# Six of eight experts with 64 slots and whole fp32 weights instead of four, expert 0 among them

## The chip, the core and the metric

The kernel runs on one core of a Trainium2 chip. The metric is the device time of one execution in microseconds (us), the median of several runs. Matrix products run on PE (TensorE), elementwise work on DVE (VectorE) and ACT (ScalarE); SP (SyncE) issues nearly all DMA transfers.

## What is computed

Two layers act on 256 context tokens and 256 image tokens, 1024 features wide. Each layer has a mixer and a feed-forward part; in the second layer only the image tokens go on, and their feed-forward part is a mixture of 8 experts of which each token uses two. The change touches this last part alone:

```python
def moe_swiglu(h, router, w1, w3, w2):
    t = h.reshape(-1, d)                                  # 256 tokens x 1024
    logits = t.astype(F32) @ router.astype(F32)
    top_logit, top_e = lax.top_k(logits, TOP_K)           # 2 of 8 experts
    gates = jax.nn.softmax(top_logit, axis=-1)
    ...
    # each expert, on the tokens that chose it: (silu(x @ w1) * (x @ w3)) @ w2
    out = jnp.zeros_like(t).at[slot_tok].add(ys * slot_gate[:, None].astype(t.dtype))
```

Per expert `w1` and `w3` are 1024 x 3584 and `w2` is 3584 x 1024, all fp32. On the given inputs the reference sends 53, 52, 64, 37, 43, 109, 114 and 40 tokens to experts 0 to 7.

## The kernel before

**Weights as a stream.** All weights come through a `Stream`: a list `todo` of blocks of 128 x 2048 fp32 (1 MB) in the order of use. `load` (L190) issues the DMA of the next block from SP's queue into a buffer; `fill` (L208) does so as long as the buffer at the head of a ring, `slots`, is free. In the expert part the ring has twelve buffers of 1 MB, and three more for a while: half of `xT` until block `n0 + LA_`, the tile `y` until block `n0 + LY`, and one that serves an earlier step. An expert has 42 blocks: 14 for each of `w1`, `w3` and `w2`, taken in units of `f` (512 of the 3584 columns), so eight experts have 336. SP has one queue: what stands behind a waiting instruction there waits too.

**Two kinds of expert.** A *big* expert has 128 slots for tokens. Its blocks are split: ACT copies a block to fp32r (`whi`, L246, two halves), DVE subtracts (`wlo`, L259, two halves), and PE multiplies in three passes with tokens on 128 columns: 12 matmuls of 512 columns a block (`up`, L1728 to L1731; `down`, L559 to L561). The raw buffer is free when both have read it. A *small* expert has 64 slots. Its blocks are not split: PE reads the raw block as fp32, two `f` or two halves of the output at once, one on the upper and one on the lower 64 columns of the array (L1719, L1753). Its raw buffer is free when PE has read it (`used`, L1706). In the profile one such fp32 matmul leaves two records.

**Who is what.** `CAP = (128, 64)` and `BIG = 4`: expert 0 always comes first, and its weights are addressed when the program is built, so they are loaded ahead; the other seven are sorted by token count on the chip, the three fullest are big, the rest small. The order is 0 (big), 4 (small), 1 (big), 5 (small), 2 (big), 6 (small), 3 (big), 7 (small), where from 1 on the number is the rank, not the expert. `gates` (L1609) ranks them on DVE after the router; `which_experts` (L1605) reads the seven numbers into SP registers, since later loads need them as addresses. If more tokens chose an expert than it has slots, `tc.If(most > 0)` (L1855) runs all experts once more as big ones, on the tokens that are left.

**The loop** (`moe`, L1661): in step n, `up` of unit n (`w1`, then `w3`), and `down` of unit n-1 (`w2`); in the last unit of an expert the tokens of the next are gathered with a 0/1 matrix (`gather`, L1677), and the result goes back through its transpose (`scatter`, L1764). A scheduler orders the instructions of each engine when the program is built.

Of the kernel before, what the change touches and what calls it, by code (L numbers as in the profile page):

```python
# [10 lines left out]
F32 = mybir.dt.float32  # L11
# [127 lines left out]
def program(tc, a, out):  # L139
# [14 lines left out]
    TAIL = (2, {1: 2, 2: 2}, {(1, 1), (2, 1), (3, 1), (4, 1)})  # L154
    NR, NH, LA = 2, 2, 1
    B4, B5 = 7, 3
    LY, LA_, NE_ = 37, 40, 5

    def bank(tag="m"):
        return ps.tile([128, 512], F32, name=nm("pm"), tag=tag, bufs=3 if tag == "m" else 1)  # L160
# [5 lines left out]
    class Halves:  # L166
# [5 lines left out]

        def __getitem__(self, i):
            return self.tiles[i[1] // self.rows][i[0], i[1] % self.rows, i[2]]

    class Stream:

# [86 lines left out]
        def take(self, la=None):  # L264
            la = LA if la is None else la
            i = self.pos[2]
            self.pos[2] += 1
            self.split_to(i + la)
            self.load_to(i + la + NR)
            self.fill()  # L270
            src, n, split, shape = self.todo[i]
            p = self.parts.pop(i)
            if not split:
                return p[:, :n].rearrange("p (j c) -> p j c", j=shape[0]) if shape else p[:, :n]
            return tuple(Halves(t, *shape) for t in p)
# [46 lines left out]
        want(*colblk('cd_w_out', c0, 256))  # L322


    CAP = (128, 64)
    BIG = 4
    SEQ = [(0, False), (4, True), (1, False), (5, True), (2, False), (6, True), (3, False), (7, True)]
    which = {}

    def units_of(seq):  # L330
# [1179 lines left out]
        V.tensor_scalar(dg, ident, rs[:, t:t + 1], None, op0=OP.mult)  # L1510
        TE.matmul(pb[:, t * 128:(t + 1) * 128], ones, dg, start=True, stop=True)
    tick(T2, False)
    pw, ww = bank(), ws.parts[n0][0][0]
    rt = ep.tile([128, 8, 8], F32, name="rt")
    nc.gpsimd.dma_start(rt, a['router'].rearrange("p (k e) -> p k e", k=8))
    cst = nw.tile([128, NROW], F32, name="cst", tag="row", bufs=1)
# [81 lines left out]
    slots, gts = [small_tile(2, 8) for i in range(2)]  # L1598
    P.iota(io64, pattern=[[0, 2], [1, 64]], base=0, channel_multiplier=0, allow_small_or_imprecise_dtypes=True)

    P.memset(lim, 8.0 * CAP[1] + 7)
    P.memset(lim[:, :BIG], 8.0 * CAP[0] + 7)
    P.memset(lim[:, 0:1], 8.0 * CAP[0] + 1e6)

    def which_experts(columns):  # L1605
        for x in columns:
# [54 lines left out]
    def moe(st, units, slots, main):  # L1661
# [15 lines left out]
        def gather(x, small):  # L1677
            sel, selr = st_q[x]
            if small:
                xe = ep.tile([128, KD, 64], F32, name=nm("xs"), tag="xe")  # L1680
                p = bank()
                for k in range(KD):
                    for i in range(2):
                        for t in range(2):
                            TE.matmul(p[:, k * 64:k * 64 + 64], h2[i][:, t, k * 128:(k + 1) * 128], selr[:, t, :64],  # L1685
                                      start=i == 0 and t == 0, stop=i == 1 and t == 1)
                A.activation(xe, p.rearrange("p (k s) -> p k s", k=KD), AF.Copy)
            else:
                xe = ep.tile([128, 2, KD, 128], F32R, name=nm("xe"), tag="xe")
                xe = [xe[:, 0], xe[:, 1]]  # L1690
                for i in range(2):
                    p = bank2()
                    for k in range(KD):
                        for t in range(2):
                            TE.matmul(p[:, k // 4, (k % 4) * 128:(k % 4) * 128 + 128], h2[i][:, t, k * 128:(k + 1) * 128],  # L1695
                                      selr[:, t, :], start=t == 0, stop=t == 1)
                    src = p.rearrange("p b (k s) -> p (b k) s", k=4)
                    (V.tensor_copy(xe[i], src) if x == 0 and i else A.activation(xe[i], src, AF.Copy))
            sT = nw.tile([128, 2, 128], F32 if small else F32R, name=nm("sT"), tag="stg" if small else "sc", bufs=1)
            p = bank()  # L1700
            for t in range(2):
                TE.transpose(p[:, t * 128:(t + 1) * 128], sel[:, t, :], ident)
            A.activation(sT, p[:, :256].rearrange("p (t s) -> p t s", t=2), AF.Copy)
            xe_q[x], st_q[x] = xe, sT

        def used():  # L1706

            st.done = st.pos[2]
            st.fill()

        def up(x, small, fs):
            p = bank()
            if small:
                n = 256 * len(fs)
                for hf in range(2):
                    w = [st.take(0) for _ in fs]
                    for k in range(4):
                        for j in range(2):
                            TE.matmul(p[64 * j:64 * j + 64, :n], xe_q[x][:, 4 * hf + k, :],  # L1719
                                      w[j][:, k, :] if len(fs) > 1 else w[0][:, k, j * 256:j * 256 + 256],  # L1720
                                      start=hf == 0 and k == 0, stop=hf == 1 and k == 3)
                    used()
                return p
            for hf in range(2):
                bh, bl = st.take()
                xh, xl = [x[:, 4 * hf:4 * hf + 4, :] for x in xe_q[x]]
                for k in range(4):
                    TE.matmul(p, xh[:, k, :], bh[:, k, :], start=hf == 0 and k == 0, stop=False)  # L1728
                    TE.matmul(p, xh[:, k, :], bl[:, k, :], start=False, stop=False)  # L1729
                for k in range(4):  # L1730
                    TE.matmul(p, xl[:, k, :], bh[:, k, :], start=False, stop=hf == 1 and k == 3)  # L1731
            return p
# [13 lines left out]
        def down(x, small, fs, at, first, last):  # L1746
            for hf in range(2 * len(fs)):
                if small:
                    w = st.take(0)
                    for i in range(2):  # L1750
                        half, c = (hf // 2, 2 * (hf % 2) + i) if len(fs) > 1 else (hf, i)
                        for j in range(2):
                            TE.matmul(ys[x][64 * j:64 * j + 64], at[:, c, 64 * half:64 * half + 64], w[:, i, j * 512:(j + 1) * 512],  # L1753
                                      start=first and hf == 0 and i == 0, stop=last and hf == 2 * len(fs) - 1 and i == 1)
                    used()
                    continue
                bh, bl = st.take()
                for i in range(2):
                    for j in range(2):
                        c = slice(j * 512, (j + 1) * 512)  # L1760
                        mm3(ys[x][j], at[0][:, 2 * hf + i, :], at[1][:, 2 * hf + i, :], bh[:, i, c], bl[:, i, c],
                            first and hf == 0 and i == 0, last and hf == 1 and i == 1)
# [52 lines left out]
        for n in range(len(units) + 1):  # L1815
            if n < len(units):
                x, small, fs, first, last = units[n]
                w = 256 * len(fs) if small else 512
                p1 = up(x, small, fs)
                s = nw.tile([128, 512], F32, name=nm("es"), tag="sq", bufs=3)  # L1820
                A.activation(s[:, :w], p1[:, :w], AF.Silu)
            if n:
                at = tr(prev, units[n - 1][1], 2 * len(units[n - 1][2]) if units[n - 1][1] else 4)
            for _ in range(min(2 if n and units[n - 1][1] else 1, len(due))):
                scatter(*due.pop(0))
            if n < len(units):
                p3 = up(x, small, fs)
                V.tensor_tensor(s[:, :w], s[:, :w], p3[:, :w], op=OP.mult)  # L1828
                if last and x in after:
                    gather(*after[x][:2])  # L1830
            if n:
                px, psmall, pfs, pfirst, plast = units[n - 1]
                if pfirst:
                    p = bank2()
                    ys[px] = p[:, 0, :] if psmall else [p[:, 0, :], p[:, 1, :]]
                down(px, psmall, pfs, at, pfirst, plast)
                if plast:
                    evac(px, psmall)
                    due += [(px, psmall, t, j) for t in range(2) for j in range(2)]
                if main and px == 0:  # L1840
                    if pfs[0] == 1:
                        gate_cols()
                    if pfs[0] == 2:
                        which_experts(range(1, NE))
                    if pfs[0] == 5:
                        sums()
                if (2 if psmall else 4) in pfs and px in after:
                    pick(*after[px][:2], slots)
            prev = s if n < len(units) else None
# [4 lines left out]
    most = nc.values_load(cnti[0:1, 0:1], min_val=0, max_val=8 * S)  # L1854
    with tc.If(most > 0):  # L1855

        V.tensor_scalar(slots[:, :, :BIG], slots[:, :, :BIG], float(CAP[0]), None, op0=OP.subtract)
        V.tensor_scalar(slots[:, :, BIG:], slots[:, :, BIG:], float(CAP[1]), None, op0=OP.subtract)
        st = Stream()
        rest = units_of([(x, False) for x in range(NE)])  # L1860
        moe_entries(st, rest, {0: 0})
        st.slots = [[slot_wp, -1, None] for _ in range(NR)] + [[slot_ep, -1, None] for _ in range(NE_)]
        st.fill()
        moe(st, rest, slots, False)
    ctx.close()


# [14 lines left out]
```

## Time and profile before

| | |
|---|---|
| median of 3 runs | 1786.39 us (1781.04 to 1786.47) |
| profiled execution, its own time | 1785.85 us |
| span, first to last instruction | 1783.6 us |
| busy in the span | PE 95%, DVE 55%, ACT 43%, POOL 7% |
| read from HBM | 471.40 MB, 266 GB/s over the span |
| mean granted TensorE clock | 0.983 |

The span is smaller than the execution's time by 2.25 us, which lie around it. PE's busy share says little by itself, because matmuls overlap: the expert part begins at about 885 us and must be read from the transfers and the waits in it.

### The profile page before, as it was taken

Reading aid. Unit: us, or ns where it says so; the run is one execution under the profiler, and the core shown is the slowest. Engines: PE = TensorE matmul, PEld = TensorE weight load, DVE = VectorE, ACT = ScalarE, POOL = GpSimd, SP = SyncE. Lnnn points to the kernel's source line nnn. Section 1 sums busy time; section 2 is a strip of 40 time slices with the busy share of each in tenths; the row PEclk is TensorE's granted clock in tenths of the full one; section 3 lists DMA queues with packets and bytes.
Section 4 is the critical chain, followed back from the end, with each engine's and each line's share of the span. In section 5 each row is a group of like instructions: output and inputs, shape, how many; then the busy total and the mean of one; then the engine's idle time right before and its main releaser. Section 6 shows DMA issues by size and latency. Waiting matters only on the chain. (4 is left out here: it accounts for less than half of the span.)

```text
span 1783.6 us, 22575 instructions
## 1 busy us (share of the span) xinstructions
PE 1700.4 (95%) x8669; PEld 1165.6 (65%) x8669; DVE 975.3 (55%) x1401; ACT 759.8 (43%) x1061; POOL 122.5 (7%) x87
## 2 busy tenths in 40 slices
PE   6898899999999998899989999999999999999997
PEld 2685577887777776777768744676446764467633
DVE  6688856333333247677678712885217852188521
ACT  3465734222221234544567602665126751267510
POOL 1433300000000000520100000000000000000000
PEclk9998999999999999999999999999999999999999
DMA  9534325223234233552879699998999979999897
GB/s 355 191 129 144 130 86 200 96 92 118 106 106 147 96 115 137 212 191 100 348 283 356 244 422 424 425 423 314 425 425 423 396 296 424 425 423 412 303 424 311
DMA packets 78739, 476.09 MB, mean 267 GB/s; under 512 B 8400, under 2 KB 12880, under 8 KB 29408
## 3 DMA queue, kind: packets, MB, share of 16 engines
q1 hardware_dynamic: 76000, 468.25, 66.8%
q0 software_dynamic: 1536, 5.28, 0.8%
q8 instruction: 70, 1.15, 0.3%
q10 hardware_dynamic: 1088, 1.05, 0.2%
q14 instruction: 45, 0.37, 0.1%
HBM read 471.40 MB, written 3.15 MB: 266 GB/s over the span
## 5 line engine op out<-in xcount | busy, mean ns | idle before, releaser
L259 DVE TENSOR_TENSOR wlo<-raw,whi 128x1024 fp32r<-128x1024 f32 (+2 forms) x414 | 487.2, 1213 | 254.3 <-ACT whi L246 245.4
L246 ACT ACTIVATE whi<-raw 128x1024 fp32r<-128x1024 f32 (+2 forms) x447 | 453.5, 1048 | 342.5 <-PE pm L560 116.4
L1719 PE MATMUL pm<-raw,xs 128*64 128x512 f32 (+1 forms) x1024 | 209.5, 542 | 0.0
L1729 PE MATMUL pm<-wlo,xe 128*128 128x512 f32 x448 | 183.8, 410 | 6.0 <-DVE wlo L259 6.0
L1728 PE MATMUL pm<-whi,xe 128*128 128x512 f32 x448 | 176.1, 398 | 4.9 <-ACT whi L246 4.9
L1719 PEld LDWEIGHTS pm<-raw,xs 128*64 128x64 f32 x1024 | 73.3, 137 | 118.7 <-issue 108.8
L1731 PE MATMUL pm<-whi,xe 128*128 128x512 f32 x448 | 123.3, 397 | 0.0
L259 POOL TENSOR_TENSOR wlo<-raw,whi 128x1024 fp32r<-128x1024 f32 (+1 forms) x33 | 80.1, 2440 | 577.5 <-ACT k L1218 486.4
L1729 PEld LDWEIGHTS pm<-wlo,xe 128*128 128x128 f32 x448 | 84.3, 188 | 45.6 <-DVE wlo L259 17.9
L1828 DVE TENSOR_TENSOR es<-es,pm 128x512 f32<-128x512 f32 (+1 forms) x44 | 29.0, 660 | 153.9 <-PE pm L1719 135.6
L1753 PE MATMUL p<-raw,ats 128*64 128x512 f32 x448 | 105.7, 597 | 0.5 <-ACT ats L1740 0.5
L1728 PEld LDWEIGHTS pm<-whi,xe 128*128 128x128 f32 x448 | 84.5, 189 | 24.7 <-ACT whi L246 8.2
L559 PE MATMUL pm<-hhi,whi 128*128 128x512 f32 x240 | 96.1, 406 | 3.8 <-ACT hhi L547 3.8
L560 PE MATMUL pm<-hlo,whi 128*128 128x512 f32 x240 | 97.3, 405 | 1.5 <-DVE hlo L548 1.4
L1731 PEld LDWEIGHTS pm<-whi,xe 128*128 128x128 f32 x448 | 84.7, 189 | 20.7
L561 PE MATMUL pm<-hhi,wlo 128*128 128x512 f32 x240 | 96.4, 402 | 0.0
L560 PE MATMUL p<-wlo,ath 128*128 128x512 f32 x224 | 92.5, 413 | 0.2 <-DVE wlo L259 0.2
L559 PE MATMUL p<-whi,ath 128*128 128x512 f32 x224 | 90.0, 402 | 0.7 <-ACT ath L538 0.7
L559 PE MATMUL p<-hhi,whi 128*128 128x512 f32 x224 | 89.0, 398 | 1.3 <-ACT hhi L538 0.7
L561 PE MATMUL p<-whi,atl 128*128 128x512 f32 x224 | 89.3, 398 | 0.0
L560 PE MATMUL p<-hlo,whi 128*128 128x512 f32 x224 | 89.1, 398 | 0.0
L561 PE MATMUL p<-hhi,wlo 128*128 128x512 f32 x224 | 88.8, 396 | 0.0
(443 smaller groups left out, 2686.6 us busy)
## 6 DMA issues: line engine op xcount, KB each, us to landing
raw<-in_moe_w_dram SPq DMA_DIRECT2D x331, 1024.0 KB, 12.1
rm<-in_mod_w_dram SPq DMA_DIRECT2D x96, 512.0 KB, 4.8
raw<-in_ffn_w_dram SPq DMA_DIRECT2D x30, 1024.0 KB, 4.8
raw<-in_ab_w_in_dram SPq DMA_DIRECT2D x7, 1024.0 KB, 6.8
raw<-in_cd_w_in_dram SPq DMA_DIRECT2D x6, 1024.0 KB, 6.5
raw<-in_ab_w_out_dram SPq DMA_DIRECT2D x4, 1024.0 KB, 4.9
raw<-in_cd_w_out_dram SPq DMA_DIRECT2D x4, 1024.0 KB, 4.9
raw<-in_ffn_w_dram SPq DMA_DIRECT2D x4, 768.0 KB, 4.2
```

The source lines that it names most:

```text
L246: x = A.activation(h, c, AF.Copy)
L259: x = low.tensor_tensor(l, r, h.bitcast(F32), op=OP.subtract)
L559: TE.matmul(p, wh, xh, start=first, stop=False)
L560: TE.matmul(p, wh, xl, start=False, stop=False)
L561: TE.matmul(p, wl, xh, start=False, stop=last)
L1719: TE.matmul(p[64 * j:64 * j + 64, :n], xe_q[x][:, 4 * hf + k, :], w[j][:, k, :] if len(fs) > 1 else w[0][:, k, j * 256:j * 256 + 256], sta ...
L1728: TE.matmul(p, xh[:, k, :], bh[:, k, :], start=hf == 0 and k == 0, stop=False)
L1729: TE.matmul(p, xh[:, k, :], bl[:, k, :], start=False, stop=False)
L1731: TE.matmul(p, xl[:, k, :], bh[:, k, :], start=False, stop=hf == 1 and k == 3)
L1753: TE.matmul(ys[x][64 * j:64 * j + 64], at[:, c, 64 * half:64 * half + 64], w[:, i, j * 512:(j + 1) * 512], start=first and hf == 0 and i = ...
L1828: V.tensor_tensor(s[:, :w], s[:, :w], p3[:, :w], op=OP.mult)
```

## The change

Expert 0 becomes small, and of the other seven only the two fullest are big: `CAP = [64, 128, 128, 64, 64, 64, 64, 64]`, in the order 0 (small), 3 (small), 1 (big), 4 (small), 2 (big), 5, 6, 7 (small). The limits for the second pass follow, and the second pass itself gets two rounds, since expert 0 can now have up to 256 - 64 tokens left. `Strips` lets PE read an unsplit block that lies in `xT`, in strips of 256 columns. `LY` and `LA_` change the blocks up to which `y` and `xT` serve as buffers. `gate_cols` and `which_experts` come after expert 0's first unit instead of its second and third. The first block is no longer split ahead of the router.

```diff
-    LY, LA_, NE_ = 37, 40, 5
+    LY, LA_, NE_ = 83, 39, 5
...
+    class Strips:
+        def __init__(self, x, shape):
+            self.x, self.n = x, shape[1] // S
+
+        def __getitem__(self, i):
+            c0, c1, _ = i[2].indices(self.n * S)
+            return self.x[i[0], i[1] * self.n + c0 // S:i[1] * self.n + c1 // S, :]
...
+            if not split and len(p.shape) == 3:
+                return Strips(p, shape)
...
-    CAP = (128, 64)
-    BIG = 4
-    SEQ = [(0, False), (4, True), (1, False), (5, True), (2, False), (6, True), (3, False), (7, True)]
+    BIG = 2
+    CAP = [64] + [128] * BIG + [64] * (7 - BIG)
+    SEQ = [(x, CAP[x] == 64) for x in (0, 3, 1, 4, 2, 5, 6, 7)]
...
-    pw, ww = bank(), ws.parts[n0][0][0]
+    pw, ww = bank(), ws.parts[n0]
...
-    P.memset(lim, 8.0 * CAP[1] + 7)
-    P.memset(lim[:, :BIG], 8.0 * CAP[0] + 7)
-    P.memset(lim[:, 0:1], 8.0 * CAP[0] + 1e6)
+    P.memset(lim, 8.0 * 64 + 7)
+    P.memset(lim[:, 1:BIG + 1], 8.0 * 128 + 7)
+    P.memset(lim[:, 0:1], 8.0 * 64 + 1e6)
...
-            sT = nw.tile([128, 2, 128], F32 if small else F32R, name=nm("sT"), tag="stg" if small else "sc", bufs=1)
+            sT = nw.tile([128, 2, 128], F32 if small else F32R, name=nm("sT"), tag="stg" if small and x != x0 else "sc", bufs=1)
...
+        def mm64(o, x, w, start, stop):
+            TE.matmul(o if len(w.shape) == 2 else o.rearrange("p (a b) -> p a b", b=S), x, w, start=start, stop=stop)
...
                 if main and px == 0:
-                    if pfs[0] == 1:
+                    if pfs[0] == 0:
                         gate_cols()
-                    if pfs[0] == 2:
                         which_experts(range(1, NE))
-                    if pfs[0] == 5:
+                    if pfs[0] == 4:
                         sums()
...
-        V.tensor_scalar(slots[:, :, :BIG], slots[:, :, :BIG], float(CAP[0]), None, op0=OP.subtract)
-        V.tensor_scalar(slots[:, :, BIG:], slots[:, :, BIG:], float(CAP[1]), None, op0=OP.subtract)
...
+        for columns, gone in ((range(NE), CAP), ([0], [128])):
```

Three places in the instruction order are needed below. A tile's name carries a number that differs from build to build.

SP's queue where expert 0 begins, before: after the first blocks of the expert part, five more loads stand ahead of the register loads of `which_experts` (L1607).

```order
L200 DMA raw_6838<-in_moe_w_2048_dram 128x2048
L200 DMA raw_7091<-in_moe_w_2048_dram 128x2048
L200 DMA raw_7113<-in_moe_w_2048_dram 128x2048
L200 DMA raw_7138<-in_moe_w_2048_dram 128x2048
L200 DMA raw_7160<-in_moe_w_2048_dram 128x2048
L200 DMA raw_7184<-in_moe_w_2048_dram 128x2048
L1607 TENSOR_LOAD cst
L1607 ISA x2
```

The same place in the changed kernel (its L1619 is L1607 of before, L210 is L200). `raw_6828` is the last block that needs no buffer to come free, the 14th; before it was `raw_6838`, the 15th.

```order
L210 DMA raw_6828<-in_moe_w_2048_dram 128x2048
L1619 TENSOR_LOAD cst
L1619 ISA x2
...
L210 DMA raw_7079<-in_moe_w_2048_dram 128x2048
L210 DMA raw_7081<-in_moe_w_2048_dram 128x2048
L1619 TENSOR_LOAD cst
L1619 ISA x2
L1868 TENSOR_LOAD cnti
L1868 ISA x2
L210 DMA raw_7091<-in_moe_w_2048_dram 128x2048
```

Six of the seven register loads now stand ahead of the 15th block's load, the seventh and that of `cnti` ahead of the 17th's.

DVE at the same place, before: the ranking of the experts (L1612 to L1627) stands between the splits of expert 0's blocks.

```order
L1617 TENSOR_TENSOR oh<-oh,g_6968 128x32
L259 TENSOR_TENSOR wlo_7133<-raw_6539,whi_7131 128x1024
L1618 TENSOR_TENSOR gt<-oh 128x16
L1621 SCALAR_TENSOR_TENSOR cst<-pm_6981,cst 128x8
L259 TENSOR_TENSOR wlo_7154<-raw_6541,whi_7152 128x1024
L1622 TENSOR_SCALAR cst<-cst 128x1
L259 TENSOR_TENSOR wlo_7155<-raw_6541,whi_7153 128x1024
L1623 MAX cst<-cst 128x8
```

The same instructions in the changed kernel:

```order
L1629 TENSOR_TENSOR oh<-oh,g_6958 128x32
L1630 TENSOR_TENSOR gt<-oh 128x16
L1633 SCALAR_TENSOR_TENSOR cst<-pm_6971,cst 128x8
L1634 TENSOR_SCALAR cst<-cst 128x1
L1635 MAX cst<-cst 128x8
L1636 MAX_INDEX cst<-cst 128x8
L1637 CAST cst<-cst 128x8
L1638 CAST cst<-cst 128x8
```

The splits between them are gone; the second cast writes the numbers that SP reads.

PE at the change from expert rank 5 to rank 6 in the changed kernel, small to small, which the kernel before does not have (L1714 transposes the 0/1 matrix for the next scatter, L1783 is the scatter of a small expert, L1724 all its other matmuls):

```order
L1714 MATMUL pm_10813<-ident,sel_10720 128x128 x2
L1724 MATMUL p_1920_10603<-raw_10679,ats_10753 64x512 x4
L1752 MATMUL pm_10868<-ident,es_10746 128x128 x2
...
L1783 MATMUL pm_10948<-zt_10911,sT_10379 128x512
L1783 MATMUL pm_10951<-zt_10911,sT_10379 128x512
...
L1783 MATMUL pm_11039<-zt_10911,sT_10379 128x512
L1783 MATMUL pm_11042<-zt_10911,sT_10379 128x512
```

The scatter of rank 5 still reads `sT_10379` after the transposes of rank 6 are made, and both lie in the one buffer `stg`; so `pm_10813`, one of three PSUM banks, is held until the last of these scatters.

## Rows read from the trace of the kernel before

**Rows 1.** The page: DMA rate in 40 equal slices of the span.

```profile
GB/s 355 191 129 144 130 86 200 96 92 118 106 106 147 96 115 137 212 191 100 348 283 356 244 422 424 425 423 314 425 425 423 396 296 424 425 423 412 303 424 311
```

**Rows 2.** Windows: length; PE, PEld, DVE, ACT, POOL busy; clock; DMA share; GB/s.

```profile
890.00:1030.00 140.00, 134.09 (x613) 101.85 (x613) 107.50 (x131) 94.26 (x108) 0.00 (x0) 0.98 0.79 297
1030.00:1200.00 170.00, 165.94 (x766) 99.85 (x763) 85.69 (x87) 73.09 (x85) 2.55 (x2) 1.00 1.01 424
1200.00:1255.00 55.00, 53.90 (x251) 35.14 (x250) 30.67 (x31) 28.25 (x33) 0.00 (x0) 1.00 0.85 334
...
1395.00:1485.00 90.00, 90.00 (x404) 62.51 (x404) 59.24 (x58) 49.88 (x58) 0.00 (x0) 1.00 0.87 347
...
1635.00:1715.00 80.00, 80.00 (x360) 51.38 (x358) 45.59 (x44) 39.90 (x47) 2.56 (x2) 1.00 0.89 350
```

**Rows 3.** Timeline of PE: expert 0 begins, then first small expert.

```profile
881.16 3.79 PE L1695 MATMUL p<-selr,h 128*128 128x128 f32 x32
...
885.17 0.48 PE L1728 MATMUL pm<-whi,xe 128*128 128x512 f32 x1
...
1018.00 13.95 PE L1719 MATMUL pm<-raw,xs 128*64 128x512 f32 x64
1031.88 0.50 PE L559 MATMUL p<-whi,ath 128*128 128x512 f32 x1
...
1037.35 0.40 PE L561 MATMUL p<-whi,atl 128*128 128x512 f32 x1
...
1053.13 7.04 PE L1753 MATMUL p<-raw,ats 128*64 128x512 f32 x32
```

**Rows 4.** Timeline of PE: the third and the fourth small expert begin.

```profile
1459.20 1.07 PE L1719 MATMUL pm<-raw,xs 128*64 128x512 f32 x2
...
1681.26 1.07 PE L1719 MATMUL pm<-raw,xs 128*64 128x512 f32 x2
```

**Rows 5.** Loads of L200 in windows 880:960, 1085:1135, 1200:1240, one row each.

```profile
DMA to landing us min/median/max: 4.7/4.9/6.7
...
DMA to landing us min/median/max: 19.2/19.6/19.7
...
DMA to landing us min/median/max: 4.7/5.6/6.8
```

**Rows 6.** Groups by line from 885 us on: busy us, mean ns, idle before.

```profile
L259 DVE TENSOR_TENSOR wlo<-raw,whi 128x1024 fp32r<-128x1024 f32 x328 | 385.5, 1220 | 99.2 <-ACT whi L246 96.5 <-PE pm L1731 2.1
L246 ACT ACTIVATE whi<-raw 128x1024 fp32r<-128x1024 f32 x328 | 331.3, 1052 | 101.4 <-PE pm L1731 83.2 <-PE p L561 13.1 <-DMA raw<-in_moe_w_dram 3.1
...
L1687 ACT ACTIVATE xs<-pm 128x512 f32<-128x512 f32 x4 | 2.3, 578 | 0.0
```

**Rows 7.** Timelines of ACT, then DVE, at the routing.

```profile
885.23 0.39 ACT L1703 ACTIVATE sT<-pm 128x256 fp32r<-128x256 f32 x1 [0.95 <-PE pm L1702]
...
889.87 1.28 ACT L1613 ACT_TABLE_LOAD   x1
...
878.44 0.17 DVE L1572 CAST ixf<-ix 128x4 f32<-128x4 uint32 x1
878.64 0.19 DVE L1573 TENSOR_TENSOR oh<-cst,ixf 128x32 f32<-128x32 f32 x1
```

**Rows 8.** Line L1607: duration ns min/median/max, first and last start.

```profile
L1607 SPq TENSOR_LOAD <-cst x7: 262/271/489, 902.7 to 907.5; - x7
```

**Rows 9.** Line L198, the last two blocks' loads in halves.

```profile
L198 SPq DMA_DIRECT2D raw<-in_moe_w_dram x4: 333/333/333, 1748.8 to 1756.0; - x4
...
DMA to landing us min/median/max: 15.4/17.2/18.9
```

**Rows 10.** Windows, columns as in Rows 2: end of the second small expert.

```profile
1310.00:1325.00 15.00, 14.42 (x106) 7.92 (x104) 0.90 (x3) 3.56 (x6) 0.00 (x0) 1.00 1.01 421
1325.00:1330.00 5.00, 2.78 (x13) 0.72 (x9) 1.26 (x2) 2.62 (x4) 0.00 (x0) 1.00 1.02 429
1330.00:1335.00 5.00, 4.98 (x15) 3.78 (x16) 3.59 (x4) 2.85 (x4) 0.00 (x0) 0.66 1.02 429
```

More of the change, by code (lines that the diff above doesn't have):

```diff
@@ L1718, in up @@
                         for j in range(2):
-                            TE.matmul(p[64 * j:64 * j + 64, :n], xe_q[x][:, 4 * hf + k, :],
-                                      w[j][:, k, :] if len(fs) > 1 else w[0][:, k, j * 256:j * 256 + 256],
-                                      start=hf == 0 and k == 0, stop=hf == 1 and k == 3)
+                            mm64(p[64 * j:64 * j + 64, :n], xe_q[x][:, 4 * hf + k, :],
+                                 w[j][:, k, :] if len(fs) > 1 else w[0][:, k, j * 256:j * 256 + 256],
+                                 hf == 0 and k == 0, hf == 1 and k == 3)
                     used()
@@ L1752, in down @@
                         for j in range(2):
-                            TE.matmul(ys[x][64 * j:64 * j + 64], at[:, c, 64 * half:64 * half + 64], w[:, i, j * 512:(j + 1) * 512],
-                                      start=first and hf == 0 and i == 0, stop=last and hf == 2 * len(fs) - 1 and i == 1)
+                            mm64(ys[x][64 * j:64 * j + 64], at[:, c, 64 * half:64 * half + 64], w[:, i, j * 512:(j + 1) * 512],
+                                 first and hf == 0 and i == 0, last and hf == 2 * len(fs) - 1 and i == 1)
                     used()
@@ L1855, in program @@
     with tc.If(most > 0):
-        V.tensor_scalar(slots[:, :, :BIG], slots[:, :, :BIG], float(CAP[0]), None, op0=OP.subtract)
-        V.tensor_scalar(slots[:, :, BIG:], slots[:, :, BIG:], float(CAP[1]), None, op0=OP.subtract)
[L1859 to L1864, printed above, removed]
+        for columns, gone in ((range(NE), CAP), ([0], [128])):
+            for x in columns:
+                V.tensor_scalar(slots[:, :, x:x + 1], slots[:, :, x:x + 1], float(gone[x]), None, op0=OP.subtract)
+            st = Stream()
+            rest = units_of([(x, False) for x in columns])
+            moe_entries(st, rest, {0: 0})
+            st.slots = [[slot_wp, -1, None] for _ in range(NR)] + [[slot_ep, -1, None] for _ in range(NE_)]
+            st.fill()
+            moe(st, rest, slots, False)
     ctx.close()
```

## The prediction

> **What bounds the kernel now.** I read the page's slices first, then windows of the expert part, then what PE needs for one block, and last what keeps a transfer from being issued.
>
> The slices show three regimes [rows 1]. Up to slice 19 (some 850 us) the rate is mostly 90 to 210 GB/s: that part waits for arithmetic, and the change hardly touches it. From there on the rate sits at 422 to 425 GB/s in most slices, with dips to 244, 314, 296 and 303. The windows put numbers on them [rows 2]. From 1030 to 1200 the transfers run at 424 GB/s without a break while PE counts as busy for 165.94 of 170 us. So in the expert part the weights are the limit, and time is lost only where the rate dips. A stretch loses its length times (1 - rate/424): 41.9 us in 890 to 1030, 11.7 in 1200 to 1255, 16.3 in 1395 to 1485, 14.0 in 1635 to 1715, together 83.9 us.
>
> Why it dips is seen in PE's price of a block. At 424 GB/s one block (1024 KB, 1.049 MB) lands every 2.473 us, an expert (42 blocks) in 103.9 us. A big expert has 12 matmuls per block; 23 steps between 1031.88 and 1037.35 make 0.238 us each [rows 3], so 2.85 us a block and 120 us an expert. A small one takes 13.95 us for the 8 blocks of the two `up` of a unit and 7.04 for the 4 of `down` [rows 3], 1.75 us a block, 73.5 us an expert, and gathers, transposes and scatters on top. A big expert is slower than its weights, a small one faster. While a big one runs, loaded blocks pile up until no buffer is free. The landing time shows it: at the end of the first small expert a load waits 19.6 us in a deep queue; as the next big one ends, 4.7 to 6.8 us, so hardly a load is ahead of it [rows 5]. A small expert then works the pile off. From one small expert to the next it takes 222.06 us [rows 4] where the weights of two need 207.7: the dip of 14 us again. The first 41.9 us are the same thing from a worse start: expert 0 is big and begins with all buffers full.
>
> **The change, part by part.** The sum is made against the profiled execution: 1785.85 us, a span of 1783.6 and 2.25 around it; the median, 1786.39, is 0.03% above. I sum when the last block lands, and add what follows it.
>
> *Start.* In SP's order 14 blocks are loaded before anything must come free (15 before, since the first was split early). PE gathers expert 0's tokens from 881.16 for 3.79 us, to 884.95 [rows 3], with as many matmuls as before. Their evacuation takes 0.58 us [rows 6], so the first `up` begins near 885.9 instead of 885.17. After two blocks, 3.5 us, two buffers are free: 889.4. But on SP six register loads now stand ahead of the 15th load and wait for the ranking. That comes after the exponential of the gates, for which ACT does the evacuation, 0.39 us for `sT`, 1.28 us of table load [rows 7] and a short activation: 887.4. DVE's chain of some 12 small instructions steps by 0.20 us [rows 7], which gives 889.8; no split stands between them any more. The seven register loads begin between 902.7 and 907.5 [rows 8]: six steps in 4.8 us, with a transfer issued among them, so some 0.7 us each; six take 4.2 us: 894.2. The first load then lands after 4.7 us in an empty queue [rows 5], at 898.9. Behind the waiting SP stand only weight loads; PE, at 1.75 us a block, comes to the 15th at 885.9 + 24.5 = 910.4, so nobody waits. Bounds: without the wait the first load goes at 889.4, 4.8 us earlier; a start as bad as now is priced among the rivals.
>
> *The blocks left.* 336 - 14 = 322, so 321 follow the first at 2.473 us: 793.8 us. Without a dip the last lands at 1692.7.
>
> *The dips.* Two big experts are left, each after a small one that has drained the pile, as in the three dips of before. Each costs 11.7 to 16.3; I take the mean of the three, 14.0: 28.0 us. At the lower end nothing, if the buffers hold the surplus. The last landing is at 1720.7.
>
> *Small after small.* Here 30 us of slack per expert (103.9 against 73.5) cover PE's other work. The one new wait: `sT` of the next expert must wait for the last scatters of the one before, and one of three PSUM banks is held so long. It can cost PE a few waits for DVE, within the slack; so 0. Without the slack the nearest row is a gather, 3.79 us [rows 3], for each of two such changes, 8 us.
>
> *Splits.* An expert made small drops 84 copies on ACT (1.052 us) and 84 subtractions on DVE (1.220 us) [rows 6], 88 and 102 us. They ran beside PE and the transfers; taking them away is worth nothing by itself beyond the start above.
>
> *`LY`, `LA_`, order of the side work.* Buffers that serve longer or shorter ahead of the first big expert, where transfers are the limit anyway: 0. The wider second pass is code that does not run.
>
> *Tail.* Before, the last half block was issued at 1756.0 and took 15.4 us [rows 9]: it landed at 1771.4, 12.2 us before the end. The last expert is small in both, so 12.2 again: a span of 1732.9, and with 2.25 a time of **1735 us**, 2.8% less.
>
> *A rule against it.* The row has 424 GB/s for 170 us [rows 2]. "DMA: Bandwidth & Descriptors" of the Trainium skill gives in its section Specifications a limit of about 358 GB/s from HBM for one core. By that figure a block would take an estimated 2.93 us, 321 of them 940 us, and the sum would come to some 1881 us, slower than before. The trace contradicts it for this kernel with one core at work, so the row decides, and I give that outcome no chance.
>
> **The rivals.**
>
> *No dips.* The starved smalls leave all buffers empty when a big expert begins, and its surplus, 42 x (2.85 - 2.473) = 16 us or 6 to 7 blocks, fits in twelve buffers. Then 28 us are saved on top: **1707 us**. Against it: the queue was at its deepest, 19.2 to 19.7 us, before the dip at 1200 too [rows 5], and the dip came.
>
> *The start or the starved experts lose more.* In 890 to 1030 my start loses what passes before the first block's 2.473 us begin, 896.4 - 890 = 6.4 us. If expert 0 loses 41.9 again [rows 2], 35 us come back: **1770 us**, and anything from 1748 on if small experts keep the queue less full than one did in 1030 to 1100. For it: they hold each buffer from issue to use, and take two at a time. Against it: the queue grew deeper all through the small experts of before [rows 5].
>
> *PE's clock.* Five of six small experts now wait for nearly every pair of blocks. In the trace the granted clock was full, 1.00, in 1310 to 1325 with PE busy for 14.42 of 15 us; after 1325 to 1330, with PE busy for 2.78 of 5 us, it fell to half, for 0.66 over the next 5 us [rows 10]. At 1.2 GHz a small expert's 73.5 us become 147, some 43 above its weights. A lost stretch here and there gives **1750 to 1780**; the gain of 51 is gone when the clock stays down for about 1.2 whole experts, and more makes it slower. Against it: a PE at half rate no longer waits, and after the row at 0.66 the clock was back. "TensorE: Matmul & The Clock Gate" of the Trainium skill, section "HAM oscillation — how this bites in real kernels", says that waits for transfers between groups of matmuls can bring the clock down again and again; the trace shows this one fall [rows 10] and 1.00 in the windows of 1030 to 1255 [rows 2], so no oscillation yet.
>
> *The second pass runs.* Expert 2 gets 64 tokens by the reference, exactly its slots, and is third of the seven. One token chooses it third, 0.0018 in the logit behind its second choice, where logits spread by 4.7. If the chip's arithmetic turns that, 65 tokens overflow 64 slots, and nine big experts follow, at 120 us or more: about **2815 us**. Before, expert 2 was big. Nothing in the trace speaks for such an error, and little can exclude it.
>
> **How the numbers follow.** 0.69 for the forecast, by itself 1724 to 1746 (dips of 9 to 18 each, start 5 either way); 0.09 for no dips; 0.10 for more lost; 0.08 for the clock, of which 0.02 slower; 0.04 for the second pass. The range 1712 to 1757 leaves out about 0.08 below (no dips) and 0.12 above. A difference of 0.3%, 5.4 us, is about what a measurement of this kernel can tell: faster 0.93, same 0.01, slower 0.06.
>
> **What would show it.** Right: weights at 424 GB/s from about 900 to 1150; two dips of some 14 us, at the ends of the two big experts; the register loads at about 890; no split of a block (L246 and L259 of before) between 885 and 1050; the last block landing near 1721 and the end 12 us later; PE less busy, with idle time put down to loads. Wrong: a dip at the start or between small experts, a granted clock under 0.97 after 1000, matmuls of three passes at the end of the program (the second pass), or no dips at all.

## The result and the profile after

The changed kernel takes **1731.8 us** (1729.69 to 1735.54, 4 runs) against 1786.43 (1781.04 to 1786.77, 4 runs), a ratio of 0.9703 [0.9678, 0.9729]: 3.0% less, where 2.8% (1735 us) was forecast. The profiled execution has a span of 1728.9 us (before 1783.6) and a mean granted clock of 0.985.

The page's slices of the changed kernel, the answer to [rows 1], DMA rate in 40 slices of the span:

```profile
GB/s 352 200 122 171 122 98 196 85 98 122 110 110 113 117 94 143 199 199 97 304 287 419 424 424 423 425 424 334 424 424 425 399 299 425 423 425 424 425 423 287
```

The weak slice after the start of the expert part is shorter, and two dips are left, 334 and 399 with 299, where there were three. In windows, the columns as in [rows 2]:

```profile
900.00:1030.00 130.00, 121.10 (x600) 47.90 (x596) 9.52 (x19) 11.27 (x21) 0.00 (x0) 1.00 1.02 421
1030.00:1150.00 120.00, 114.12 (x515) 74.94 (x516) 72.86 (x71) 62.73 (x70) 0.00 (x0) 0.99 1.01 424
1150.00:1185.00 35.00, 35.00 (x167) 28.08 (x166) 29.20 (x28) 23.92 (x26) 0.00 (x0) 1.00 1.00 409
1185.00:1220.00 35.00, 33.90 (x148) 18.10 (x146) 11.76 (x13) 10.28 (x14) 0.00 (x0) 1.00 0.83 327
...
1340.00:1390.00 50.00, 50.00 (x214) 38.25 (x212) 42.25 (x41) 35.51 (x39) 0.00 (x0) 1.00 0.99 394
1390.00:1420.00 30.00, 30.00 (x147) 23.37 (x148) 20.99 (x22) 16.71 (x20) 0.00 (x0) 1.00 0.90 320
1420.00:1500.00 80.00, 78.90 (x388) 33.12 (x386) 11.59 (x14) 10.69 (x16) 2.56 (x2) 0.99 0.96 401
1500.00:1600.00 100.00, 92.17 (x428) 35.61 (x426) 6.87 (x10) 5.33 (x10) 0.00 (x0) 0.96 1.01 424
1600.00:1700.00 100.00, 85.66 (x387) 29.68 (x383) 6.87 (x10) 5.33 (x10) 0.00 (x0) 0.99 1.01 425
```

With the prediction's formula (length times 1 - rate/424.5, since the last two rows have 424 and 425) the start loses 1.1 us from 900 on, the first dip (1150 to 1220) 1.3 + 8.0 = 9.3, the second (1340 to 1500) 3.6 + 7.4 + 4.4 = 15.4. After the second dip the rows hold 424 and 425 GB/s until the weights end, and PE is the one that waits: its idle time is the largest in the last row.

SP's loads in the second dip (1400:1420), then in 1500:1600, the answers to [rows 5]:

```profile
DMA to landing us min/median/max: 5.2/6.3/7.4
...
DMA to landing us min/median/max: 18.7/19.6/19.8
```

The queue is nearly empty in the dip and eight loads deep behind it: 19.6 us, with 2.467 us between two landings (70 of them, from 1464.2 to 1636.9). Where expert 0 begins, the register loads (columns as in [rows 8]) and the first load behind them:

```profile
L1619 SPq TENSOR_LOAD <-cst x7: 264/266/472, 883.4 to 888.3; - x7
...
887.46 4.22 SPq L210 DMA_DIRECT2D raw<-in_moe_w_dram  x6
```

PE's timeline where the experts change (L1697 gathers for a small expert, L1707 for a big one):

```profile
874.93 3.76 PE L1697 MATMUL pm<-selr,h 128*128 128x64 f32 x32
...
1180.51 1.76 PE L1697 MATMUL pm<-selr,h 128*128 128x64 f32 x15
...
1278.65 2.00 PE L1707 MATMUL p<-selr,h 128*128 128x128 f32 x16
...
1403.82 2.09 PE L1697 MATMUL pm<-selr,h 128*128 128x64 f32 x18
```

A gather stands near the end of the `up` of the expert before it (1278.65 is the second half of the big expert's gather), so these rows cut PE's time into experts: 98.1 us for a small one between two big ones, 125.2 for a big one. The weights of either take 42 x 2.467 = 103.6. How the two share their 223.3 us depends on the cut. At the first `up` matmul of each (L1724 small, L1743 big) it gives 94.3 and 129.1:

```profile
1193.19 1.07 PE L1724 MATMUL pm<-raw,xs 128*64 128x512 f32 x2
...
1287.44 0.50 PE L1743 MATMUL pm<-whi,xe 128*128 128x512 f32 x1 [1.49 <-ACT whi L256]
...
1416.53 0.64 PE L1724 MATMUL pm<-raw,xs 128*64 128x512 f32 x1
```

### The profile page after: what moved, and what is told of

Its sections match the earlier page's. It is cut to its first block, busy times and chain, and to the rows that moved or that the text cites. A ratio compares the mean times of both kernels' runs of the same rounds, so it can differ in the third digit from the quotient of the medians.

```text
span 1728.9 us, 21387 instructions
## 1 busy us (share of the span) xinstructions
PE 1618.4 (94%) x8369; PEld 1028.2 (59%) x8369; DVE 768.1 (44%) x1214; ACT 580.8 (34%) x872; POOL 115.9 (7%) x81
## 5 line engine op out<-in xcount | busy, mean ns | idle before, releaser
L269 DVE TENSOR_TENSOR wlo<-raw,whi 128x1024 fp32r<-128x1024 f32 (+2 forms) x254 | 298.8, 1210 | 200.8 <-ACT whi L256 192.9
L256 ACT ACTIVATE whi<-raw 128x1024 fp32r<-128x1024 f32 (+2 forms) x285 | 289.4, 1045 | 287.8 <-PE pm L572 116.9
L1724 PE MATMUL pm<-raw,xs 128*64 128x512 f32 (+1 forms) x1504 | 321.5, 551 | 28.3 <-DMA raw<-in_moe_w_dram 27.3
L1724 PEld LDWEIGHTS pm<-raw,xs 128*64 128x64 f32 x1504 | 113.4, 138 | 216.0 <-issue 150.4
L1724 PE MATMUL p<-raw,ats 128*64 128x512 f32 x672 | 165.3, 598 | 4.4 <-DMA raw<-in_moe_w_dram 3.9
L1724 PEld LDWEIGHTS p<-raw,ats 128*64 128x64 f32 x672 | 47.8, 136 | 92.9 <-issue 75.7
L1744 PE MATMUL pm<-wlo,xe 128*128 128x512 f32 x224 | 92.6, 413 | 3.1 <-DVE wlo L269 3.1
L1743 PE MATMUL pm<-whi,xe 128*128 128x512 f32 x224 | 88.4, 400 | 3.0 <-ACT whi L256 3.0
L452 PE MATMUL pm<-rm,sc 128*32 128x256 f32 x768 | 61.2, 405 | 11.1 <-DMA rm<-in_mod_w_dram 9.7
L571 PE MATMUL pm<-ah,whi 128*128 128x512 f32 x176 | 70.2, 402 | 0.0
L572 PE MATMUL pm<-al,whi 128*128 128x512 f32 x176 | 69.6, 397 | 0.0
L573 PE MATMUL pm<-ah,wlo 128*128 128x512 f32 x176 | 69.0, 396 | 0.0
```

The source lines that it names most:

```text
L256: x = A.activation(h, c, AF.Copy)
L269: x = low.tensor_tensor(l, r, h.bitcast(F32), op=OP.subtract)
L452: TE.matmul(mst[2][32 * i:32 * i + 32, :256], sc[:, k, :], r[:, i * 256:(i + 1) * 256], start=k == 0, stop=k == 7)
L571: TE.matmul(p, wh, xh, start=first, stop=False)
L572: TE.matmul(p, wh, xl, start=False, stop=False)
L573: TE.matmul(p, wl, xh, start=False, stop=last)
```

## The experiments

**Theory 1**: in the expert part the time is that of the weights at 424 GB/s plus the stretches in which the queue of loads runs empty; the change removes the bad start and one dip. **Theory 2**: each expert that is made small gives back its own work on PE, ACT and DVE, the same for each.

### The two halves of the change apart

First from the kernel before, expert 0 left big:

```diff
-    BIG = 4
-    SEQ = [(0, False), (4, True), (1, False), (5, True), (2, False), (6, True), (3, False), (7, True)]
+    BIG = 3
+    SEQ = [(0, False), (4, True), (1, False), (5, True), (2, False), (3, True), (6, True), (7, True)]
```

> The kernel before, with one expert fewer in 128 slots: expert 0 keeps 128 slots and split weights, the two fullest of the others are big, five are small (order 0, 4, 1, 5, 2, 3, 6, 7 of the ranks). Theory 1 (the time is that of the weight transfers plus the stretches in which the queue of loads stands still): the slow start of expert 0 stays (41.9 us lost there), and one of the three later dips (11.7, 16.3 and 14.0 us) is gone, so about 14 us less than before, 1772 us. Theory 2 (each expert that is made small gives back its own work, so the 54.6 us of the change are shared by the two experts): 27 us less, 1759 us.

Measured: 1767.93 us (1765.19 to 1771.37), 0.9919 [0.9901, 0.9937], 4 us from theory 1 and 9 from theory 2; the time alone hardly tells them apart. Its windows at the places of [rows 2]:

```profile
890.00:1030.00 140.00, 134.54 (x615) 101.71 (x615) 104.71 (x125) 88.41 (x101) 0.00 (x0) 0.98 0.80 300
1200.00:1255.00 55.00, 53.90 (x248) 34.46 (x247) 29.07 (x29) 23.84 (x28) 0.00 (x0) 1.00 0.86 338
1395.00:1485.00 90.00, 90.00 (x405) 59.79 (x405) 55.07 (x54) 47.20 (x56) 2.55 (x2) 1.00 0.88 347
1635.00:1715.00 80.00, 68.77 (x299) 22.35 (x295) 6.18 (x9) 4.35 (x8) 0.00 (x0) 1.00 1.01 425
```

The start and two dips are as they were; the last, 14.0 us, is gone. The other half, from the changed kernel, expert 0 left small:

```diff
-    BIG = 2
+    BIG = 3
-    SEQ = [(x, CAP[x] == 64) for x in (0, 3, 1, 4, 2, 5, 6, 7)]
+    SEQ = [(x, CAP[x] == 64) for x in (0, 4, 1, 5, 2, 6, 3, 7)]
```

> The changed kernel with one more big expert: the three fullest of experts 1 to 7 have 128 slots (order 0, 4, 1, 5, 2, 6, 3, 7), expert 0 stays small. Theory 1: one more dip, of 14 to 16 us, and nothing else: 1746 to 1748 us. Theory 2: half of the change is undone, 27 us more, 1759 us. Together with the run that keeps expert 0 big it tells whether the two halves of the change are worth the same.

Measured: 1746.64 us (1744.96 to 1749.34), 0.9794 [0.9779, 0.9810]. A third dip is back, and the start is as good as in the changed kernel:

```profile
900.00:1030.00 130.00, 122.88 (x612) 48.95 (x610) 9.52 (x19) 11.28 (x21) 0.00 (x0) 1.00 1.02 421
...
1600.00:1670.00 70.00, 70.00 (x320) 46.89 (x320) 40.92 (x39) 34.97 (x41) 0.05 (x1) 1.00 0.87 334
```

Expert 0 small gains 2.1%, some 37 us; one later expert small gains 0.8%, some 14 to 16 us. The halves are not alike, so theory 2 falls; together they make the 3.0% within the noise.

### No big expert at all

```diff
-    BIG = 2
+    BIG = 0
...
+    P.memset(lim, 1e9)
```

> The changed kernel with 64 slots for all eight experts and the second pass never run; it leaves out the tokens beyond 64 of the two fullest experts. Theory 1: no dips are left, the 26 us that the changed kernel still loses in its two dips are gone, 1705 us, and the transfers run at 424 GB/s from the first expert's blocks to the last. Theory 2: two more experts give 27 us each, 1677 us.

Measured: 1707.91 us (1706.79 to 1710.19), 0.9581 [0.9566, 0.9595]: 24 less than the changed kernel, whose two dips were 24.7, and far from theory 2's 1677. First two windows, then PE's gathers for two experts in turn, then PE's waits from the one gather to the other (us in total, times, longest):

```profile
1150.00:1300.00 150.00, 132.84 (x644) 53.06 (x643) 10.32 (x18) 8.68 (x17) 0.00 (x0) 0.98 1.01 424
1300.00:1600.00 300.00, 260.80 (x1229) 98.79 (x1230) 19.01 (x29) 15.79 (x30) 0.00 (x0) 0.99 1.01 424
...
1156.76 1.42 PE L1695 MATMUL pm<-selr,h 128*128 128x64 f32 x11
...
1260.48 1.75 PE L1695 MATMUL pm<-selr,h 128*128 128x64 f32 x14
...
PE pm L1722 <- DMA raw<-in_moe_w_dram: 11.1, 11, 1.3
...
PE p L1722 <- DMA raw<-in_moe_w_dram: 0.9, 2, 0.4
```

A small expert takes 103.7 us here, as long as its weights, and 12.0 of them are waits for loads. So PE needs some 92 us for one (the next takes 103.5, of which 9.5 are such waits: 94), and its slack is 10 to 12 us, not the 30 of the prediction. From that a finer theory 1: a big expert that PE begins with nothing piled up exceeds its weights by 125.2 - 103.6 = 21.6 us; 9.3 of them were lost in the first dip, so the buffers took some 12. This is an estimate, and by the other cut it would be 129.1 - 103.6 - 9.3 = 16. A small and a big one in steady turn need 98.1 + 125.2 = 223.3 us against 207.2, and the 16 us between would be lost whatever the buffers hold; this sum is the same by either cut.

### Two small experts between the big ones

```diff
-    SEQ = [(x, CAP[x] == 64) for x in (0, 3, 1, 4, 2, 5, 6, 7)]
+    SEQ = [(x, CAP[x] == 64) for x in (0, 3, 1, 4, 5, 2, 6, 7)]
```

> The changed kernel with its two big experts two places apart (order 0, 3, 1, 4, 5, 2, 6, 7 rather than 0, 3, 1, 4, 2, 5, 6, 7); the work is the same. Theory 1, with what the trace of the changed kernel adds: the second dip lost 16 us against 10 in the first, and if that is because only one small expert stands between them and TensorE has not caught up by then, a second small one between them brings it down to about 10: 1726 us. Rival: a dip costs what one big expert's work exceeds its transfers by, whatever stands before it: 1732 us.

Measured: 1727.55 us (1725.38 to 1730.22), 0.9687 [0.9672, 0.9701], an interval that overlaps that of the change. So both ran once more on one chip:

> The changed kernel itself, once more beside the run below on one chip, because the two were timed on different occasions and their intervals overlap. 1731 us.

> The changed kernel with its big experts two places apart, once more. Theory 1 (the second dip shrinks from 16 us to 9): 4 to 7 us less than the run above. Rival (no difference beyond the scatter of runs): within 2 us of it.

Measured: the changed kernel 1733.07 us (1732.16 to 1734.62), 0.9721 [0.9707, 0.9734]; with the big ones apart 1725.75 (1725.19 to 1726.75), 0.9680 [0.9666, 0.9693]. The intervals are apart by now. The dips of the latter:

```profile
1150.00:1185.00 35.00, 35.00 (x167) 28.09 (x166) 28.96 (x27) 23.92 (x26) 0.00 (x0) 1.00 0.99 409
1185.00:1220.00 35.00, 33.90 (x149) 18.11 (x149) 11.76 (x13) 10.53 (x14) 0.00 (x0) 1.00 0.82 324
1470.00:1500.00 30.00, 30.00 (x133) 23.65 (x132) 26.03 (x25) 22.07 (x25) 0.00 (x0) 1.00 1.01 414
1500.00:1530.00 30.00, 30.00 (x150) 18.46 (x150) 12.75 (x12) 12.63 (x16) 0.00 (x0) 1.00 0.76 288
```

They lose 1.3 + 8.3 and 0.7 + 9.7 us: the second is now like the first. What stands ahead of a big expert sets its dip.

### Two buffers fewer

```diff
-    LY, LA_, NE_ = 83, 39, 5
+    LY, LA_, NE_ = 83, 39, 3
```

> The changed kernel with two buffers fewer (NE_ = 3 rather than 5). Theory 1: two blocks fewer are loaded ahead (4.9 us later at the end), the first dip, which comes on an empty pile, grows by two blocks (4.9 us), and the second, which comes 208 us of weights but some 223 us of TensorE's work after the first, does not: 1741.6 us, with the second dip at 15 to 17 us still. Rival: each dip depends on the buffers alike: 1746.5 us. Second rival: the buffers have no part in it, only the later start shows: 1736.7 us.

Measured: 1741.33 us (1739.70 to 1742.05), 0.9764 [0.9748, 0.9780]. The same windows as those of the changed kernel:

```profile
1150.00:1185.00 35.00, 35.00 (x154) 27.67 (x153) 29.82 (x29) 26.03 (x29) 0.00 (x0) 1.00 0.94 363
1185.00:1220.00 35.00, 35.00 (x168) 20.67 (x167) 14.55 (x16) 14.41 (x18) 0.00 (x0) 1.00 0.76 295
1340.00:1390.00 50.00, 50.00 (x215) 38.77 (x215) 43.34 (x42) 35.90 (x39) 0.00 (x0) 1.00 1.01 415
1390.00:1420.00 30.00, 30.00 (x147) 24.17 (x147) 23.44 (x24) 19.86 (x23) 0.00 (x0) 1.00 0.90 328
1420.00:1500.00 80.00, 78.90 (x360) 31.96 (x358) 14.66 (x17) 12.61 (x19) 2.55 (x2) 1.00 0.94 389
```

The first dip grew from 9.3 to 5.1 + 10.7 = 15.8 us, the second stayed, 15.4 to 1.1 + 6.8 + 6.7 = 14.6. The time is theory 1's; of the dips, the growth of 6.5 us stands against its 4.9, and 14.6 against its 15 to 17. The two dips do not depend on the buffers alike.

### The splits put back

For each block of the small experts 3 to 7 a copy and a subtraction, whose results nothing reads:

```diff
+        def used(x=0):
+            if x:
+                (h,), (l,) = st.pair(1)
+                A.activation(h, m5, AF.Copy)
+                V.tensor_tensor(l, m5, h.bitcast(F32), op=OP.subtract)
...
-                    used()
+                    for _ in fs:
+                        used(x)
...
-                    used()
+                    used(x)
```

> The changed kernel with one copy on ACT and one subtraction on VectorE of 128 x 1024 (about 1.05 and 1.22 us) put back for each block of the five small experts 3 to 7, 210 of each where the change took away 168; they read the tile m5 and their results are not used. Theory 1: work on ACT and VectorE beside transfers that are the limit costs nothing: 1732 us, within 5. Theory 2 (the change gained by the removed work): some 54 us come back or more, 1786 us.

Measured: 1761.02 us (1760.49 to 1762.19), 0.9878 [0.9862, 0.9894], between the two: both theories missed. In a second run each pair reads the block in use in place of `m5`:

```diff
+        def used(x=0, w=()):
+            for b in w if x else ():
...
+                b = b[:, :2, :512]
+                A.activation(h, b, AF.Copy)
+                V.tensor_tensor(l, b, h.bitcast(F32), op=OP.subtract)
```

> As the run with the splits put back, 210 copies on ACT and 210 subtractions on VectorE over experts 3 to 7, but each reads half of the block that TensorE is using, so that it cannot run long before that block has landed. In the run before, which read a tile that was always ready, the instruction order had them in heaps: VectorE was busy for 98.4 of the 100 us from 1500 to 1600 and for 8.4 of the next 100, and TensorE waited for it. Theory 1 (they cost nothing where they are spread beside the transfers; it was the heaps that cost 29 us): 1732 us, within 5. Rival (the work costs a small expert its slack wherever it stands, since each silu, product and evacuation waits behind it): 1755 to 1765 us again.

Measured: 1733.05 us (1732.53 to 1735.14), 0.9714 [0.9696, 0.9731], as without them. Two windows of the first run, then of the second (PE, PEld, DVE, ACT and POOL busy):

```profile
1500.00:1600.00 100.00, 74.68 (x354) 29.30 (x352) 98.41 (x91) 85.46 (x88) 0.00 (x0) 0.85 0.91 369
1600.00:1700.00 100.00, 95.67 (x462) 35.47 (x460) 8.37 (x12) 6.31 (x12) 0.00 (x0) 1.00 1.01 424
```

```profile
1500.00:1600.00 100.00, 92.57 (x448) 36.74 (x446) 58.50 (x55) 49.53 (x55) 0.00 (x0) 1.00 1.01 424
1600.00:1700.00 100.00, 89.36 (x396) 34.44 (x394) 54.79 (x51) 46.52 (x49) 0.00 (x0) 0.98 1.01 424
```

Within the heap of the first run, DVE's timeline and PE's waits from 1500 to 1600 (us in total, times, longest):

```profile
1539.83 36.43 DVE L1722 TENSOR_TENSOR wlo<-m,whi 128x1024 fp32r<-128x1024 f32 x32
1576.15 0.71 DVE L1847 TENSOR_TENSOR es<-es,pm 128x512 f32<-128x512 f32 x1
...
PE pm L1756 <- DVE es L1847: 25.3, 2, 14.6
```

The same work cost 28 us in heaps, and nothing spread out: in the heap DVE is busy for 98.41 of 100 us, a silu's product stands behind 32 subtractions, and PE is down to 74.68 us. By the landings of the loads 13.5 us were lost there. The rest was lost in the two dips, some 8 to 9 us more in each, where PE waits 5.8 us for an evacuation on ACT that it does not wait for in the changed kernel. "TensorE: Matmul & The Clock Gate" of the Trainium skill calls ACT and DVE strict first-in, first-out (section "Architectural detail: the array is 16× 32×32, not 1× 128×128"). The heap agrees, with 36.43 us of subtractions ahead of one product of 0.71. So here it is not the amount of work on ACT and DVE that counts, but what stands behind it.

### Big units between small ones

```diff
+    for b, s0 in ((1, 3), (2, 5)):
+        i = min(n for n, u in enumerate(UNITS) if u[0] in (b, s0))
+        sm, bg = [[u for u in UNITS if u[0] == x] for x in (s0, b)]
+        UNITS[i:i + 11] = [(sm if k == 's' else bg).pop(0) for k in 'sbbsbbsbsbb']
```

(`SEQ`, gathers, scatters, buffers for the gathered tokens, `LY` and the splitting ahead follow the new order.)

> The changed kernel with the same eight experts of the same sizes, but each big expert's units of 512 columns laid between those of a small one (small, big, big, small, big, big, small, big, small, big, big), in the order 0, then 3 with 1, then 4, then 5 with 2, then 6 and 7. Theory 1, made sharper by the earlier runs (from the gather of a small expert to the next TensorE needs some 92 us, a big one 125, the weights of either come in 104; the buffers hold some 12 us of surplus, and the rest is a dip): a pair needs 217 us against 207, an excess of 10 that fits in the buffers, so neither dip is left: 1708 us, as with no big expert at all. Rival: a big expert's work costs its dip wherever it stands: 1728 to 1732 us.

Measured: 1729.30 us (1723.34 to 1731.58), 0.9693 [0.9673, 0.9712]; theory 1's number missed, the rival's range holds. PE's longest waits in the first pair (951.4 to 1176.6):

```profile
PE pm L1747 <- ACT whi L256: 5.0, 3, 1.7
PE pm L1756 <- DVE es L1847: 2.3, 3, 0.9
PE pm L1748 <- DVE wlo L269: 1.8, 2, 1.0
```

Around the changes from small to big PE waits for a split or a silu's product; a pair takes 225 us, not 217, and by the landings of the loads 6.3 us are lost behind the first pair and some 18 in and after the second. Unmixed, this order is that of the runs with the big ones apart, which took 1725.75 and 1727.55 us: mixing one with one gained nothing over it. So a big expert was spread over two small ones (the edit against the kernel above; `SEQ` and the buffers follow again):

```diff
-        sm, bg = [[u for u in UNITS if u[0] == x] for x in (s0, b)]
-        UNITS[i:i + 11] = [(sm if k == 's' else bg).pop(0) for k in 'sbbsbbsbsbb']
+        sm, bg = [[u for u in UNITS if u[0] in x] for x in ((s0, s0 + 1), (b,))]
+        UNITS[i:i + 15] = [(sm if k == 's' else bg).pop(0) for k in 'ssbbssbbsbbbsss']
```

> The same eight experts once more, each big one laid between the units of two small ones: 0, then 3 and 4 with 1, then 5 and 6 with 2, then 7 (units small, small, big, big, small, small, big, big, small, big, big, big, small, small, small). In the run that mixed one with one, a pair took 225 to 229 us, not the 217 summed, since TensorE waits some 10 us for ACT and VectorE at the changes from one kind to the other; that is 18 to 22 us over the weights, more than the buffers' 12, so dips stayed. Theory 1: a group of three needs 125 + 2 x 92 + 8 for the changes, 317 us against 311 of weights; the excess of 6 fits in the buffers, no dip is left: 1708 us. Rival: the changes cost more than the spread gives, and it ends at 1728 to 1732 us again.

Measured: **1720.64 us** (1717.92 to 1723.10), 0.9645 [0.9627, 0.9664], the fastest kernel that computes everything. The dips have become shallow, but not gone:

```profile
1200.00:1360.00 160.00, 155.53 (x719) 75.09 (x719) 42.83 (x49) 35.60 (x47) 2.53 (x2) 0.98 0.98 409
1360.00:1400.00 40.00, 36.75 (x154) 20.25 (x150) 17.11 (x17) 17.88 (x20) 0.00 (x0) 0.96 1.01 424
1400.00:1600.00 200.00, 191.99 (x901) 110.23 (x900) 91.24 (x90) 72.81 (x86) 2.55 (x2) 1.00 0.96 399
```

They lose 5.8 and 12.0 us. The direction is theory 1's, the number is not; why the second group still loses 12 was not settled. PE waits for splits and silu products in this kernel too, 24.4 us between 900 and 1600.

## Why the prediction was right, point by point

**The bound.** Right: weights at 424 GB/s wherever the queue is full. One thing was read too simply: in the kernel before, from the second pair on, PE sets the pace, with 222 us for a pair [rows 4], and there a dip is PE's surplus, not a queue that could have been kept fuller. The prediction's price of a big expert, 120 us from its matmuls alone, was low too: PE takes 125.2 (129.1 by the other cut).

**The start.** It was to lose 6.4 us in place of 41.9, with the 15th block landing at 898.9, 17.7 after the gather. It was issued at 887.46, ahead of the last register load, and landed at 892.18, 17.3 after the gather at 874.93. The place of the wait and its length were right (889.8 and 4.2 make 894.0 in the prediction, not 894.2); the whole expert part lay 6 us earlier than in the profile of before. Part of that at least is scatter between executions. In the 13 profiles of all these kernels the first gather begins between 873.69 and 881.16, and the forecast was built on the latest of them. The kernel with expert 0 left big, whose program up to the experts is that of before, also begins to gather early:

```profile
875.27 1.00 PE L1695 MATMUL p<-selr,h 128*128 128x128 f32 x7
```

The start's worth was the largest term, 41.9 - 6.4 = 35.5, and the two halves apart show it: 37 us. What within it does the work was not separated. Expert 0's smaller work on PE, its missing splits and the new place of the register loads came together in every run, and the splits put back later left expert 0 out. SP's longest waits, in the kernel before from 885 to 1030 and in the changed one from 880 to 1030, tell what held the loads:

```profile
SPq L200 <- DVE wlo L259: 85.6, 28, 8.8
...
SPq L210 <- DMA raw<-in_moe_w_dram: 78.1, 41, 2.1
```

Before, they waited for the subtractions that free the buffers, with PE busy for 134.09 of 140 us [rows 2]; in the changed kernel, for earlier loads. That speaks for PE's work as the cause, without showing it alone.

**The blocks.** 2.467 us for one in the place of 2.473: 791.9 us for 321, 1.9 less.

**The dips.** Right in number and place; 14.0 each was a mean over unlike cases. They are 9.3 and 15.4 by the windows, 24.7 together for 28.0; by the landings of single loads 26.6, with 4.1 lost elsewhere, which the sum did not have. That the total is near is in part luck: one dip came out below 14 and one above. What the step "the dips" lacked is where a dip's size comes from: behind a starved small expert, a big one's surplus less what the buffers take (two buffers fewer: 6.5 us more); behind a small one that had a pile to work off, PE's surplus over a pair, 16 us, whatever the buffers.

**Small after small.** The step "30 us of slack per expert (103.9 against 73.5)" was off in size. It set only the matmuls with weights against the weights; gathers, transposes, scatters and what lies between bring PE to 92 us, and the slack to 12. The term, 0, still held, since 12 was enough: no dip came between small experts. Had the slack been put at 12, it would have told that one small expert can't work off what a big one leaves.

**Splits.** Worth nothing by themselves: held for experts 3 to 7, with 210 pairs put back at 1733.05 us, on the condition that they are not bunched in front of what PE waits for.

**Tail.** 13.4 us (from 1715.5 to 1728.9) for 12.2. The sum: 892.2 + 791.9 + 30.7 lost (26.6 and 4.1) = 1714.8 for the last landing (1715.5 in the trace), and a span of 1728.9, against 1732.9 forecast. The early start (-6.7), the blocks (-1.9), the losses (+2.7) and the tail (+1.2) make up the difference, within 1 us. An early start that is in part scatter and losses that were put too small offset one another in part; that is luck, and no term was off by more than 7 us.

**The rivals.** No dips: they came. More lost: no. Clock: it was 0.96 to 1.00 in the windows of the changed kernel, although PE waited for loads in the small experts. The 0.96 (1500 to 1600) is below the 0.97 that the prediction named as a sign of being wrong. It comes from single falls to the lower level, 1.2 GHz, as in this window (its clock is the last figure but two); in the 6 us before it PE was busy for 5.16 at 1.00, so the rows do not tell what set it off:

```profile
1532.00:1537.00 5.00, 5.00 (x16) 1.33 (x16) 0.75 (x1) 0.00 (x0) 0.00 (x0) 0.66 1.01 419
```

The weights came at 424 GB/s over those 100 us, so the falls cost nothing that the rows show. The repeated falls at waits for transfers that "TensorE: Matmul & The Clock Gate" of the Trainium skill tells of in its section "HAM oscillation — how this bites in real kernels" did not come. The second pass did not run. The limit of 358 GB/s from "DMA: Bandwidth & Descriptors" of the Trainium skill was not met, as the row had it; the same page's table of measured transfers by one core alone (section "Bandwidth") has 425 GB/s for 16 MB, which is what the last row of the windows shows.

## What to carry to other kernels

Where weights stream and stages differ in what they ask of TensorE, add up for each stage all of TensorE's work from gather to gather, not the large matmuls alone, and set it against the stage's transfers; the surplus goes into the buffers, and what doesn't fit is lost. Then the order of the stages is worth time: two light ones between the heavy ones gave 7 us, and each heavy one laid among two light ones some 11 to 12 in all (5 to 7 more than the heavy ones merely apart), for the same work. Work that is hidden on another engine stayed free here only as long as it wasn't queued in one heap ahead of something that the bottleneck waits for.

## What the hardware showed that was not expected

- With all experts small, the rate of 424 GB/s held from 1150 to 1600 us without a dent, with eight loads of 1 MB waiting in the queue (19.2 to 21.1 us from issue to landing between 1300 and 1600).
- The part ahead of the experts differs by some 4 to 6 us between executions of the same instructions: gathers began at 874.93 and 878.64 in two profiles of the changed kernel, and at 881.16 and 875.27 in two kernels with the same program up to there. That is as much as the 5.4 us that the prediction took as the least difference to be told apart.
- The same 210 pairs of instructions on ACT and DVE cost 28 us in heaps and nothing spread out. In the 100 us in which DVE was busiest, PE was idle for a quarter of the time, and its granted clock was 0.85.
